# Hybrid decoder layer on one core: rows of chunks 1 to 3 turned by VectorE instead of TensorE, their norm applied at the projections' outputs

## The chip, the cores and the metric

The kernel runs on one core of a Trainium2 chip. The metric is the device time of one execution in microseconds (us), taken as the median of the runs. The core has TensorE for matmuls (PE in the profile; its weight loads stand apart as PEld), VectorE (DVE), ScalarE (ACT), GpSimd (POOL) and SyncE (SP), which here only issues transfers. A transfer is issued by an instruction in the stream of SP, ACT or POOL and is carried out by 16 DMA engines that all of them share. Each engine works through its own instructions in the order in which they were written down.

## The reference

One layer of a decoder, batch 1, 2048 positions, width 1024, all in float32:

```python
h = rms_norm(x, attn_norm_g)                 # over 1024 channels, gain per channel
z = h @ w_in                                 # 1024 -> 2304 columns
q, k, v = z[:512], z[512:640], z[640:768]    # 8 heads of 64, 2 key/value heads
gate_b, gate_c, xc = the last 3 x 512 columns
q, k = rms_norm(q, q_norm_g), rms_norm(k, k_norm_g)
y_attn = sliding-window attention (window 128, one learned sink per head)
y_conv = gate_b * short_conv(gate_c * xc, conv_w)       # causal, 3 taps
x = x + concat(rms_norm(y_attn), rms_norm(y_conv)) @ w_out
x = x + square(relu(rms_norm(x, mlp_norm_g) @ w_up)) @ w_down     # 1024 -> 4096 -> 1024
```

The norm of a row is one number per position, 1/sqrt(mean(x^2) + 1e-6). Called rs below, it may be multiplied into the row ahead of `w_in`, or into the products behind it.

## The kernel before

The positions are cut into four chunks of 512 (`CH`), each of four tiles of 128 positions (`NT`). To keep float32 accuracy every matmul is done as three: each operand is split into a high part (rounded to TensorE's fast float32 format by ScalarE) and a low part (the rest, by VectorE), and `mm3` adds high by high, high by low, low by high (lines 266 to 268).

`mixers(c, ...)` does one chunk of the first half of the layer. Two strands run side by side in it. The one is attention, tile by tile: `scores`, `softmax`, `values`. The other is the generator `besides`, from which `fill(n)` takes n steps between the pieces of attention. Its steps in order: the attention half of the output projection left from the chunk before; two `conv_pair` (matmuls `pc`, `px`, `pb`, with h as the moving operand, so the output has channels on partitions and positions along the row); the convolution half of `out_projection` (`pout<-w_wo,yt`, 96 matmuls), between whose steps `prepare` makes the next chunk's h; then `project_qkv` of the next chunk (`pz`, with h as the stationary operand, so the output has positions on partitions). A planner lays every engine's instructions out in order ahead of time; it goes by the place in the program, shifted by `ahead(i)` by amounts that depend on the chunk, and by when it believes an instruction's inputs to be ready.

h of a chunk lies channels on partitions, in eight blocks k of [128 channels, 512 positions], as a high and a low tile (tags `h0`, `h1`, one buffer each). The next chunk's h can therefore be written only when the last matmul of `conv_pair` (`pb`) has read this chunk's.

For chunk 0 (lines 435 to 540) TensorE turns the raw rows, the gain `g_in` is multiplied in when they are copied out, and rs comes in behind the matmuls: `rs0` as ScalarE's scale where positions lie on partitions, `rs0_row` (VectorE, line 804) where they lie along the row, `rs0_2` (its square) in the norm of the convolution's output.

For chunks 1 to 3 `prepare` (line 363) does four tiles of 128 positions one after the other. `fetch(t)` loads [128, 1024] rows on SP's queue into one of two buffers (line 369), ScalarE squares and sums them (line 275), GpSimd makes rs (lines 190 and 191), and VectorE multiplies by rs and the gain row (line 282). `transposed` (line 288) then lets TensorE turn them in two groups of four 128x128 blocks into the one bank `tr` (line 294), ScalarE copies out the high part (line 298) and VectorE subtracts for the low part (line 299). The rows are already normalized, so `conv_pair` and `project_qkv` copy their products out on ScalarE (lines 802 and 602).

The second half of the layer (products `u` at line 1426 and `d` at line 1533) works on blocks of 512 with seven products in place of eight (Strassen). Its inputs of chunks 2 and 3 are made by `prepare_rest` during the `u` products: `load_turned` loads blocks whose 32x32 squares VectorE's transpose puts in place (`turned`, lines 323 and 324), and the row of rs for them comes by way of DRAM: `rs_out` (line 338) writes it, line 1230 reads it back to all partitions.

Of the kernel before, what the change touches and what calls it, by code (L numbers as in the profile page):

```python
# [70 lines left out]
STEPS = 3  # L71
TS = 32
REST = 7
LATER = 250
# [28 lines left out]
def hymba_layer(  # L103
# [46 lines left out]
    ]  # L150
    rs_dram = [dram.tile([CH], F32, name=f"rs_dram{c}") for c in range(NCHUNK)]
    wds_dram = [[dram.tile([P, 2, BW], F32, name=f"wds{g}_{i}") for i in range(2)] for g in range(NCG // 2)]

    def bank(tag, name):
        return psum.tile([P, 512], F32, tag=tag, name=name, bufs=BANKS[tag])
# [127 lines left out]

    def norm(xt, gb, name):

        scaled(xt, norm_stats(xt, name), gb)

    def transposed(xt, dst, t, name, tag="tr"):

        for kk in range(0, KD, 4):  # L290
            with ahead(9):
                pt = bank(tag, f"pt_{name}_{kk}")
                for j in range(4):
                    nc.tensor.transpose(pt[:, j * P : (j + 1) * P], xt[:, (kk + j) * P : (kk + j + 1) * P], ident)
                p3 = pt.rearrange("p (k t) -> p k t", k=4)
                dh = dst[0][:, kk : kk + 4, t * P : (t + 1) * P]
                dl = dst[1][:, kk : kk + 4, t * P : (t + 1) * P]
                nc.scalar.copy(dh, p3)
                nc.vector.tensor_tensor(dl, p3, dh.bitcast(F32), op=ALU.subtract)
            yield  # L300

    def raised(xt, dst, name, tag="tr"):
# [8 lines left out]

    def load_turned(xb, src, r0, jj):

        for pg in range(4):
            rows = src[r0 : r0 + BW].rearrange("(q i) (k c) -> i k q c", i=TS, k=2)
            c0 = jj * P + pg * TS
            nc.sync.dma_start(
                xb[pg * TS : (pg + 1) * TS].rearrange("p (k q c) -> p k q c", k=2, c=TS), rows[:, :, :, c0 : c0 + TS]
            )

    def turned(xb, k, dst, g, rs_row):

        nc.vector.transpose(dst, xb[:, k * BW : (k + 1) * BW])
        nc.vector.scalar_tensor_tensor(dst, dst, g, rs_row, op0=ALU.mult, op1=ALU.mult)

# [10 lines left out]
    def rs_out(c):  # L336

        nc.gpsimd.dma_start(
            rs_dram[c].rearrange("(t p) -> p t", p=P), rs_x1[:, c * NT : (c + 1) * NT]
        )  # L340
# [21 lines left out]

    def prepare(src, r0, gb, dst, name):

        xs = []

        def fetch(t):
            xt = row("xt", f"xt_{name}_{t}", 2)
            nc.sync.dma_start(xt, src[r0 + t * P : r0 + (t + 1) * P, :])
            with ahead(8):  # L370
                norm(xt, gb, f"{name}_{t}")
                xs.append(xt)

        fetch(0)
        fetch(1)
        yield
        for t in range(NT):
            yield from transposed(xs[t], dst, t, f"{name}_{t}")
            if t + 2 < NT:
                fetch(t + 2)  # L380

# [161 lines left out]
    with tc.tile_pool(name="mix_small", bufs=1) as mix_small, tc.tile_pool(name="mix", bufs=1) as mix:  # L543
# [9 lines left out]
        v_diff = mix.tile([P, KVH * DH], F32, name="v_diff")  # L553
        def project_qkv(c, h, z):

# [37 lines left out]
            for pc, t in ((0, 0), (0, 1), (1, 0), (0, 2), (0, 3), (1, 1), (1, 2), (1, 3)):  # L593
                n = 256 if pc else AW
                ps = bank("mm", f"pz{c}_{pc}_{t}")[:, :n]
                hk = lambda s, k, t=t: h[s][:, k, t * P : (t + 1) * P]
                wk = (lambda s, k: w4[s][:, k, :]) if pc else (lambda s, k: both[k // (KD // 2)][s][:, k % (KD // 2), :])
                for k in range(KD):
                    mm3(ps, lambda s, k=k: hk(s, k), lambda s, k=k: wk(s, k), k == 0, k == KD - 1)
                    if (k % 2 or not pc) and k < KD - 1:  # L600
                        yield
                nc.scalar.copy(z[t][:, pc * AW : pc * AW + n], ps)
                if pc and not t:
                    qk_norm(c * NT, z[0])
                yield
# [171 lines left out]

        def conv_pair(c, h, j, yt, ssc):

# [17 lines left out]
            for i in range(2):  # L797
                ps = bank("mm", f"pc_{nm}_{i}")
                yield from group(hl, ps, i)
                g = pool.tile([P, CHP], F32, tag="s2", name=f"u_{nm}_{i}", bufs=4)  # L800
                if c:
                    nc.scalar.copy(g[:, 2 : CH + 2], ps)
                else:
                    nc.vector.tensor_tensor(g[:, 2 : CH + 2], ps, rs0_row, op=ALU.mult)
                gc.append(g)
                yield
# [132 lines left out]

        def besides(c, before, h, yt, rc, x1, h_next, z_next):  # L940
# [12 lines left out]
            if c + 1 < NCHUNK:  # L953
                h_next += parts(pool, "h", f"h{c + 1}")
                steps = prepare(xf, (c + 1) * CH, g_row[0], h_next, f"a{c + 1}")
            else:
                steps = prepare_mlp(gain_row(mlp_norm_g, "g_mlp"))
            for i, _ in enumerate(steps):
                yield
                for j in range(STEPS):  # L960
                    next(out, None)
                    yield
                    if (i, j) == PC:
# [7 lines left out]
                        with tc.high_priority(offset=SOON):  # L971
                            if c:
                                nc.vector.tensor_copy(ms, pc[:, :NT])
                                rsqrt(rc, ms)
                            else:
                                nc.vector.tensor_tensor(ms, pc[:, :NT], rs0_2, op=ALU.mult)
                                rsqrt(rc, ms)
                                nc.gpsimd.tensor_tensor(rc, rc, rs0, op=ALU.mult)
            yield from out
            if c + 1 < NCHUNK:  # L980
                yield from project_qkv(c + 1, h_next, z_next)
            else:
                begin_mlp()

        def mixers(c, before, h, z):

# [3 lines left out]
            stage[0] = c  # L990
            at, yt, x1, h_next, z_next = [], [], [], [], []
            ra = small.tile([P, NT], F32, tag="ra", name=f"ra{c}", bufs=2)
            rc = small.tile([P, NT], F32, tag="rc", name=f"rc{c}", bufs=2)
            steps = besides(c, before, h, yt, rc, x1, h_next, z_next)
            left = out_projection(c, 0, at, ra, x1)

# [46 lines left out]

            return rest(), h_next, z_next

# [42 lines left out]
        left = iter(())  # L1088
        for c in range(NCHUNK):
            left, h, z = mixers(c, left, h, z)  # L1090
        for _ in left:
# [481 lines left out]
```

## Time and profile before

| | |
|---|---|
| median of 3 runs | 1937.9 us (1937.33 to 1943.99) |
| the profiled execution's own time | 1940.91 us |
| its span, first to last instruction | 1939.2 us |
| granted TensorE clock | 0.997 |
| PE, PEld, DVE, ACT, POOL busy | 99%, 82%, 62%, 43%, 14% of the span |

In the profile, a row of a group gives the line, the engine, the operation, what is written and read, the shape and the count; behind the first bar the busy time and the mean ns of one; behind the second the idle time of that engine right before these instructions and what ended it. Matmuls are pipelined and their ends are modelled, so a PE that is busy 99% still says little: how far apart the starts of its instructions lie says more. Issues of transfers are not counted as busy time. For a transfer, "to landing" is the time from its issue to the signal that it is complete.

### The profile page before, as it was taken

What the parts mean: (1) busy time and instruction counts of PE and PEld (TensorE: products, weight loads), DVE (VectorE), ACT (ScalarE), POOL (GpSimd) and SP (SyncE); (2) the same over time, 40 slices, a digit from 0 to 9 for tenths busy, and PEclk for the clock granted to TensorE, in tenths of its full rate; (3) what the DMA queues carried; (4) which work ended last, traced back from release to release, by engine and by line L of the source; (5) the groups of instructions that cost most, each with busy time, mean ns of one, the idle gap of its engine ahead of it and who ended that gap; (6) DMA issues with size and microseconds to landing.
All of it is one profiled execution on the core that took longest, in us unless ns stands there. A gap on an engine that the chain in (4) does not pass through costs nothing.

```text
span 1939.2 us, 24806 instructions
## 1 busy us (share of the span) xinstructions
PE 1919.0 (99%) x9025; PEld 1597.5 (82%) x9025; DVE 1202.8 (62%) x1872; ACT 837.4 (43%) x1593; POOL 273.5 (14%) x473
## 2 busy tenths in 40 slices
PE   9999999999999999999999999999999999999999
PEld 9888887888888788788877888888888888888887
DVE  4885657447556768888878766666544334448541
ACT  6564444335344436445465555554422332232320
POOL 2122212302221202222200111111000000100000
PEclk9999999999999999999999999999999999999999
DMA  9774854464474788877666544437964446766631
GB/s 334 273 264 140 313 207 174 183 251 152 181 258 159 261 293 259 237 222 245 229 219 202 179 151 148 162 122 293 381 219 142 150 160 233 262 230 215 210 136 54
DMA packets 240634, 412.25 MB, mean 213 GB/s; under 512 B 51704, under 2 KB 147968, under 8 KB 228736
## 3 DMA queue, kind: packets, MB, share of 16 engines
q1 hardware_dynamic: 211824, 335.15, 50.6%
q0 software_dynamic: 15424, 51.40, 7.2%
q10 hardware_dynamic: 13264, 24.13, 3.3%
q8 instruction: 71, 1.16, 0.2%
q14 instruction: 51, 0.42, 0.1%
HBM read 284.78 MB, written 125.83 MB: 212 GB/s over the span
## 4 chain that ended last, share of the span: by engine, by line
PE 85%; issue 5%; DVE 3%; DMA 3%; ACT 2%; POOL 2%; SPq 1%; POOLq 0%; DVEq 0%; ACTq 0%
PE d L1533 31%; PE u L1426 24%; PE pout L266 2%; PE pout L268 2%; PE pout L267 2%; PE pz L266 2%; PE pz L267 2%; PE pz L268 2%; PE pc_c L266 2%; PE px_c L266 2%; PE px_c L268 2%; PE px_c L267 2%; PE pc_c L268 2%; PE pc_c L267 2%; PE psc_b L664 1%
## 5 line engine op out<-in xcount | busy, mean ns | idle before, releaser
L1426 PE MATMUL u<-op_x,wop 128*128 128x512 f32 x2688 | 614.5, 390 | 5.9 <-DVE wop L416 4.4
L1533 PE MATMUL d<-op_w,op_f 128*128 128x512 f32 x2688 | 609.4, 389 | 0.0
L1426 PEld LDWEIGHTS u<-op_x,wop 128*128 128x128 f32 x2688 | 504.7, 188 | 115.2 <-DVE wop L416 7.4
L1533 PEld LDWEIGHTS d<-op_w,op_f 128*128 128x128 f32 x2688 | 504.5, 188 | 104.8
L397 DVE TENSOR_TENSOR op_f<-op_f 128x1024 fp32r<-128x1024 f32 x112 | 136.9, 1225 | 233.8 <-ACT op_f L396 233.3
L396 ACT CAST op_f<-op_f 128x1024 fp32r<-128x1024 f32 x112 | 118.0, 1054 | 349.0 <-DMA op_f<-fop 343.1
L415 ACT CAST wop<-wu 128x512 fp32r<-128x512 f32 x156 | 96.3, 621 | 91.7 <-PE u L1426 88.1
L416 DVE TENSOR_TENSOR wop<-wu,wop 128x512 fp32r<-128x512 f32 x156 | 111.4, 715 | 36.5 <-ACT wop L415 18.8
L1162 POOL DMA_DIRECT2D fop<-s x96 | 52.3, 545 | 440.6 <-DVE s L1165 433.9
L1168 DVE TENSOR_TENSOR u<-u,u 128x512 f32<-128x512 f32 x128 | 87.7, 685 | 20.3 <-PE u L1426 20.3
L397 DVE TENSOR_TENSOR op_w<-raw,op_w 128x1024 fp32r<-128x1024 f32 x56 | 68.4, 1222 | 29.8 <-ACT op_w L396 29.6
L396 ACT CAST op_w<-raw 128x1024 fp32r<-128x1024 f32 x56 | 58.9, 1054 | 48.6 <-PE d L1533 26.6
L1174 ACT ACTIVATE u<-u 128x512 f32<-128x512 f32 x64 | 40.5, 634 | 53.9 <-DVE u L1168 52.0
L681 ACT ACTIVATE sc_b<-sc_b,ngm_b 128x128 f32<-128x128 f32 x128 | 49.8, 394 | 26.5 <-DVE ngm_b L678 26.5
L713 POOL TENSOR_SCALAR_AFFINE_SELECT pp_b<-pp_b 128x512 fp32r<-128x512 f32 x60 | 41.4, 702 | 119.1 <-ACT pp_b L706 64.1
L1375 POOL DMA_DIRECT2D wds<-raw x16 | 8.6, 536 | 332.9 <-DVE raw L1373 332.9
L415 ACT CAST wop<-wu_s 128x512 fp32r<-128x512 f32 x64 | 39.5, 621 | 36.2 <-PE u L1426 28.8
L266 PE MATMUL pout<-w_wo,yt_c 128*128 128x512 f32 x128 | 52.9, 413 | 0.0
L268 PE MATMUL pout<-w_wo,yt_c 128*128 128x512 f32 x128 | 52.4, 409 | 0.0
L267 PE MATMUL pout<-w_wo,yt_c 128*128 128x512 f32 x128 | 51.7, 404 | 0.0
L266 PE MATMUL pout<-w_wo,at_b 128*128 128x512 f32 x128 | 50.2, 394 | 0.2 <-DVE x L891 0.2
L267 PE MATMUL pout<-w_wo,at_b 128*128 128x512 f32 x128 | 50.0, 390 | 0.3 <-DVE w_wo L249 0.3
(255 smaller groups left out, 3126.1 us busy)
## 6 DMA issues: line engine op xcount, KB each, us to landing
op_f<-fop SPq DMA_DIRECT2D x112, 512.0 KB, 4.2
raw<-in_w_down_dram SPq DMA_DIRECT2D x72, 512.0 KB, 4.2
wu<-in_w_up_dram SPq DMA_DIRECT2D x128, 256.0 KB, 3.9
w_wo<-wo SPq DMA_DIRECT2D x24, 1024.0 KB, 6.8
fop<-s POOLq DMA_DIRECT2D x96, 256.0 KB, 2.8
fop<-u ACTq DMA_DIRECT2D x64, 256.0 KB, 2.2
op_x<-xop SPq DMA_DIRECT2D x28, 512.0 KB, 6.6
w_q<-qkv SPq DMA_DIRECT2D x24, 512.0 KB, 6.1
```

Source lines behind the costliest of these rows:

```text
L266: nc.tensor.matmul(ps, st(0), mv(0), start=first, stop=False)
L267: nc.tensor.matmul(ps, st(0), mv(1), start=False, stop=False)
L268: nc.tensor.matmul(ps, st(1), mv(0), start=False, stop=last)
L396: nc.scalar.copy(op[:, 0], raw)
L397: nc.vector.tensor_tensor(op[:, 1], raw, op[:, 0].bitcast(F32), op=ALU.subtract)
L415: splits.append(nc.scalar.copy(hi, blk).ins)
L416: nc.vector.tensor_tensor(lo, blk, hi.bitcast(F32), op=ALU.subtract)
L681: nc.scalar.activation(sc[:, hd, :], sc[:, hd, :], AF.Exp, bias=ngm[:, hd : hd + 1], accum_out=den[:, hd : hd + 1])
L1162: eng.dma_start(fop_dram[tb][ORDER_DOWN.index(i)][n // 2][:, n % 2], b)
L1168: return nc.vector.tensor_tensor(dst, ps, b, op=ALU.add).ins
L1426: nc.tensor.matmul(pt, wops[i][:, a, k, :], xops[tb, p][k // 2][:, b, k % 2, :], start=p not in GOES_ON and k + j == 0, stop=k + j == NB + ...
L1533: nc.tensor.matmul(ps[tb][j], fs[tb][:, a, k, j * P : (j + 1) * P], w[:, b, k, :], start=first and p not in GOES_ON and k + n == 0, stop=l ...
```

## The change

For chunks 1 to 3 the raw rows now go the way of chunk 0, with VectorE in place of TensorE. `load_turned` brings 512 positions by 128 channels in four transfers of 128 KB in pieces of 32 elements; tiles jj = 0 and 1 are issued on SP's queue, 2 and 3 on ScalarE's, once the two `xt` buffers have been read. Per block k, VectorE turns [128, 512] into one half of a new tile `gb`, ScalarE makes the high part times the gain `g_in[k]`, VectorE the low part. rs comes from `stats`, run between the steps of the `conv_pair`s (one step in `STATS` = 9): half rows [128, 512] of the next chunk are loaded on ScalarE's queue into the other half of `gb`, squared and summed in place by ScalarE, and GpSimd makes rs and its square; the square goes to DRAM and comes back as a row to all partitions. `conv_pair` multiplies `pc` by this row on VectorE, for all chunks; `project_qkv` scales by rs on ScalarE; the norm of the convolution's output takes in rs. All rows that go by way of DRAM are now stored partition by partition (`rs_out` too) and read with a step of 4 elements. `norm`, `transposed` and the gain row's load are gone.

```diff
+STATS = 9
-    def transposed(xt, dst, t, name, tag="tr"):
...
-                    nc.tensor.transpose(pt[:, j * P : (j + 1) * P], xt[:, (kk + j) * P : (kk + j + 1) * P], ident)
...
-                nc.scalar.copy(dh, p3)
-                nc.vector.tensor_tensor(dl, p3, dh.bitcast(F32), op=ALU.subtract)
...
-    def load_turned(xb, src, r0, jj):
+    def load_turned(xb, src, r0, jj, eng=None):
...
-            nc.sync.dma_start(
+            (eng or nc.sync).dma_start(
...
         nc.vector.transpose(dst, xb[:, k * BW : (k + 1) * BW])
-        nc.vector.scalar_tensor_tensor(dst, dst, g, rs_row, op0=ALU.mult, op1=ALU.mult)
+        d3, r3 = dst.rearrange("p (t q) -> p t q", t=NT), rs_row.rearrange("p (q t) -> p t q", t=NT)
+        nc.vector.scalar_tensor_tensor(d3, d3, g, r3, op0=ALU.mult, op1=ALU.mult)
...
         nc.gpsimd.dma_start(
-            rs_dram[c].rearrange("(t p) -> p t", p=P), rs_x1[:, c * NT : (c + 1) * NT]
+            rs_dram[c].rearrange("(p t) -> p t", p=P), rs_x1[:, c * NT : (c + 1) * NT]
         )
...
+    def prepare(c, dst, gb):
+        xts = {}
+        def fetch(jj):
+            xts[jj] = row("xt", f"xt_a{c}_{jj}", 2)
+            load_turned(xts[jj], xf, c * CH, jj, nc.scalar if jj > 1 else nc.sync)
         fetch(0)
         fetch(1)
         yield
+        for jj in range(NB):
+            for k in (jj, jj + NB):
+                xt = xts[jj][:, (k // NB) * BW : (k // NB + 1) * BW]
+                with ahead(9):
+                    dh, dl = (d[:, k] for d in dst)
+                    st = gb[:, k // NB]
+                    nc.vector.transpose(st, xt)
+                    nc.scalar.activation(dh, st, AF.Copy, scale=g_in[k])
+                    nc.vector.scalar_tensor_tensor(dl, st, g_in[k], dh.bitcast(F32), op0=ALU.mult, op1=ALU.subtract)
+                yield
+            if jj + 2 < NB:
+                fetch(jj + 2)
+    def stats(c, rs, gb):
+        xr = gb[:, 1]
+        def fetch(t, i):
+            r = c * CH + t * P
+            nc.scalar.dma_start(xr, xf[r : r + P, i * CH : (i + 1) * CH])
+        with tc.issue_after(z_in[-1]) if c == 1 else nullcontext():
+            fetch(0, 0)
+        yield
         for t in range(NT):
...
+            for i in range(2):
+                nc.scalar.activation(xr, xr, AF.Square, scale=D**-0.5, accum_out=ss[:, i : i + 1])
+                if t + i < NT:
+                    fetch(t + i, 1 - i)
+                if i:
+                    nc.gpsimd.tensor_scalar(ss[:, :1], ss[:, :1], EPS, ss[:, 1:], op0=ALU.add, op1=ALU.add)
+                    nc.gpsimd.tensor_tensor(rs[0][:, t : t + 1], ss[:, :1], mhalf[:, :1], op=ALU.pow)
+                yield
+        nc.gpsimd.tensor_tensor(rs[1], rs[0], rs[0], op=ALU.mult)
+        nc.gpsimd.dma_start(rs2_dram[c].rearrange("(p t) -> p t", p=P), rs[1])
...
-                nc.scalar.copy(z[t][:, pc * AW : pc * AW + n], ps)
+                nc.scalar.activation(z[t][:, pc * AW : pc * AW + n], ps, AF.Copy, scale=rs[:, t : t + 1])
...
-                if c:
-                    nc.scalar.copy(g[:, 2 : CH + 2], ps)
-                else:
-                    nc.vector.tensor_tensor(g[:, 2 : CH + 2], ps, rs0_row, op=ALU.mult)
+                t3 = lambda a: a.rearrange("p (t q) -> p t q", t=NT)
+                nc.vector.tensor_tensor(t3(g[:, 2 : CH + 2]), t3(ps), rs2_row, op=ALU.mult)
...
+            gb = pool.tile([P, 2, CH], F32, tag="gb", name=f"gb{c}", bufs=1)
+            rs2_row = rs0_row.rearrange("p (t q) -> p t q", t=NT)
+            if c:
+                nc.sync.dma_start(gb[:, 0], rs2_dram[c].partition_broadcast(P))
+                rs2_row = gb[:, 0].rearrange("p (q t) -> p t q", t=NT)
...
             for j in range(2):
-                yield from conv_pair(c, h, j, yt, ssc)
+                for i, _ in enumerate(conv_pair(c, h, j, yt, ssc, rs2_row)):
+                    if i % STATS == STATS - 1:
+                        next(sums, None)
+                    yield
+            for _ in sums:
+                pass
...
-                            if c:
-                                nc.vector.tensor_copy(ms, pc[:, :NT])
-                                rsqrt(rc, ms)
-                            else:
-                                nc.vector.tensor_tensor(ms, pc[:, :NT], rs0_2, op=ALU.mult)
-                                rsqrt(rc, ms)
-                                nc.gpsimd.tensor_tensor(rc, rc, rs0, op=ALU.mult)
+                            nc.vector.tensor_tensor(ms, pc[:, :NT], rs[1], op=ALU.mult)
+                            rsqrt(rc, ms)
+                            nc.gpsimd.tensor_tensor(rc, rc, rs[0], op=ALU.mult)
...
-        g_row = [gain_row(attn_norm_g, "g_attn")]
```

More of the change, by code (lines that the diff above doesn't have):

```diff
@@ L151, in hymba_layer @@
     rs_dram = [dram.tile([CH], F32, name=f"rs_dram{c}") for c in range(NCHUNK)]
+    rs2_dram = [dram.tile([CH], F32, name=f"rs2_dram{c}") for c in range(NCHUNK)]
     wds_dram = [[dram.tile([P, 2, BW], F32, name=f"wds{g}_{i}") for i in range(2)] for g in range(NCG // 2)]
@@ L776, in attn_rstd, with conv_pair @@
             rsqrt(dst, ms)
-        def conv_pair(c, h, j, yt, ssc):
+        def conv_pair(c, h, j, yt, ssc, rs2_row):
             nm = f"c{c}_{j}"
@@ L1042, in rest @@
                     yield
-            return rest(), h_next, z_next
+            return rest(), h_next, z_next, rs_next
         z = []
```

43 lines of the change are left out of this document (13 added, 30 removed).

## The prediction

> **What bounds the kernel.** I read the page's busy times first, then a table by stretches for the part that the change touches (before about 48 us chunk 0's products start the layer, after 690 us only the second half runs), then who waited for whom on TensorE. A row of the table gives the stretch, its length, and the busy time of each engine in it.
>
> ```profile
> span 1939.2 us, 24806 instructions
> PE 1919.0 (99%) x9025; PEld 1597.5 (82%) x9025; DVE 1202.8 (62%) x1872; ACT 837.4 (43%) x1593; POOL 273.5 (14%) x473
> 48.00:690.00 642.00, 634.93 (x3240) 531.46 (x3239) 417.52 (x835) 295.03 (x794) 134.81 (x226) 1.00 0.60 217
> 123.00:156.00 33.00, 31.95 (x174) 26.62 (x174) 29.89 (x59) 20.66 (x53) 8.01 (x14) 1.00 0.80 275
> 219.00:295.00 76.00, 76.00 (x372) 63.70 (x371) 44.87 (x93) 33.02 (x103) 9.22 (x21) 1.00 0.64 249
> 295.00:329.00 34.00, 32.00 (x170) 26.17 (x169) 25.50 (x53) 17.82 (x50) 9.73 (x15) 1.00 0.47 155
> 466.00:500.00 34.00, 33.04 (x179) 27.17 (x178) 28.75 (x57) 19.08 (x52) 8.87 (x13) 1.00 0.59 202
> ```
>
> TensorE bounds it: in the 642 us of the mixers it is without work for 7. The stretches at 123, 295 and 466 us are those in which the next chunk's h is made; there TensorE is idle for 1 to 2 us, and VectorE is nearly as full as TensorE (29.89 of 33 us at 123, 28.75 of 34 at 466). Between them, as at 219, VectorE has 31 of 76 us to spare. What TensorE waited for, and what the parts that go and come cost:
>
> ```profile
> PE u L1426 <- DVE wop L416: 4.4, 4, 2.9
> PE pt_a L294 <- DVE h_h L299: 1.8, 4, 1.2
> PE po_b L752 <- POOL pp_b L713: 0.3, 1, 0.3
> PE pout L267 <- DVE w_wo L249: 0.3, 1, 0.3
> ```
>
> ```profile
> L294 PE MATMUL pt_a<-ident,xt_a 128*128 128x128 f32 x96 | 14.8, 277 | 4.0 <-DVE h_h L299 1.8 <-DVE ms_b L775 1.2 <-DVE xt_a L282 1.0
> L294 PEld LDWEIGHTS pt_a<-ident,xt_a 128*128 128x128 f32 x96 | 11.2, 140 | 9.0 <-DVE h_h L299 3.7 <-DVE ms_b L775 2.0 <-DVE xt_a L282 1.5
> L282 DVE SCALAR_TENSOR_TENSOR xt_a<-xt_a,rs_a,g_attn 128x1024 f32<-128x1024 f32 x12 | 16.1, 1343 | 5.4 <-POOL rs_a L191 5.4
> L299 DVE TENSOR_TENSOR h_h<-pt_a,h_h 128x512 fp32r<-128x512 f32 x24 | 16.5, 689 | 3.8 <-ACT h_h L298 3.4
> L323 DVE STREAM_TRANSPOSE st_m<-xt_r 128x512 f32<-128x512 f32 x16 | 10.9, 696 | 0.0
> L249 DVE SCALAR_TENSOR_TENSOR w_wo<-raw_wo,g_y,w_wo 128x512 fp32r<-128x512 f32 x16 | 11.6, 745 | 0.0
> L804 DVE TENSOR_TENSOR u_c<-pc_c,rs_row 128x512 f32<-128x512 f32 x4 | 2.8, 688 | 2.2 <-PE pc_c L268 2.2
> L275 ACT ACTIVATE junk_a<-xt_a 128x1024 bf16<-128x1024 f32 x12 | 12.7, 1061 | 6.1 <-DMA xt_a<-in_x_dram 5.4 <-DVE y_c L821 0.4 <-issue 0.2
> L275 ACT ACTIVATION_READ_ACCUMULATOR junk_a<-xt_a 128x1 f32 x12 | 2.3, 190 | 0.0
> L298 ACT CAST h_h<-pt_a 128x512 fp32r<-128x512 f32 x24 | 14.0, 583 | 21.5 <-PE pt_a L294 21.3
> L802 ACT COPY u_c<-pc_c 128x512 f32<-128x512 f32 x12 | 7.1, 589 | 12.6 <-PE pc_c L268 12.4
> L248 ACT ACTIVATE w_wo<-raw_wo,g_y 128x512 fp32r<-128x512 f32 x16 | 10.8, 724 | 0.1
> L766 ACT ACTIVATE o_b<-o_b 128x512 f32<-128x512 f32 x16 | 10.0, 627 | 6.4 <-DVE at_b L765 6.3
> ```
>
> **What TensorE gets back.** The 96 transposes go, in 24 groups of four. What a group takes of TensorE's time is not its 277 ns each, which overlap, but the step between starts:
>
> ```profile
> 123.51 0.39 PE L268 MATMUL pout<-w_wo,yt_c 128*128 128x512 f32 x1
> 123.74 0.60 PE L294 MATMUL pt_a<-ident,xt_a 128*128 128x128 f32 x4
> 124.09 0.48 PE L266 MATMUL pout<-w_wo,yt_c 128*128 128x512 f32 x1
> ```
>
> A matmul of 512 columns holds the place for 0.23 us (123.51 to 123.74), the group of four for 0.35 (to 124.09): 24 x 0.35 = 8.4 us. With them go their waits, 4.0 us on the matmul row; the weight loads waited 9.0, partly beside running matmuls, so 4.0 to 9.0, and I take 4.0. These waits had one cause: a product for the next chunk stood in TensorE's order ahead of ready matmuls and needed a chain over GpSimd, VectorE and the single bank `tr`. In the new order nothing on TensorE touches h before `project_qkv`, so the next thing that can be late is h itself, below.
>
> **The stores by way of DRAM.** One more hole may close. The longest wait in the list above, 2.9 us for `wop`, stands at 776 us, far behind the mixers:
>
> ```profile
> L338 POOL DMA_DIRECT2D rs_dram<-rs_x x2: 851/930/1009, 565.5 to 768.9; - x2
> DMA to landing us min/median/max: 9.0/10.2/11.4
> fop<-s POOLq DMA_DIRECT2D x96, 256.0 KB, 2.8
> 768.91 0.85 POOL L338 DMA_DIRECT2D rs_dram<-rs_x  x1 [0.29 <-POOL rs_x L191]
> 778.19 0.69 DVE L1165 TENSOR_TENSOR s<-f,u 128x512 f32<-128x512 f32 x1 [7.00 <-DMA fop<-s]
> 779.54 0.73 PE L1426 MATMUL u<-op_x,wop 128*128 128x512 f32 x2 [2.93 <-DVE wop L416]
> ```
>
> `rs_out` stores 2 KB as 512 single elements at 768.91 and needs about 10 us to land. The `fop` store issued right behind it, of a kind that lands in 2.8 us, lets VectorE go only at 778.19, 7.0 us late; `wop` stands behind that on VectorE, and TensorE loses 2.93. Stored partition by partition the same row is 128 pieces of 4 elements, a quarter as many. If the delay goes with the pieces, 7.0 becomes 1.8 us, below the 7.0 - 2.9 = 4.1 us that were hidden, and the hole closes: between 0 and 2.9 us won, and I take 2.9, since the only slow store of its kind stands right behind this one. Sum of the gains: 8.4 + 4.0 + 2.9 = 15.3 us.
>
> **What the other engines get.** Per chunk, VectorE loses 4 x 1.343 + 8 x 0.689 = 10.9 us (L282, L299) and gets 8 transposes at 0.696 and 8 low parts at 0.745 (same operation and place as L249), 11.5 us, all in the stretch where h is made, and 4 x 0.688 = 2.8 us in `conv_pair` for what ScalarE copied. The 2.8 lie where 31 of 76 us are free. The +0.6 at 123 us make VectorE's work 29.89 + 0.6 = 30.5 us, while TensorE's, without 8 x 0.35 and the idle 33.00 - 31.95, falls to 33 - 2.8 - 1.0 = 29.2: 1.3 us of that gain cannot be had unless VectorE's work moves out of the stretch. At 295 and 466 us VectorE stays below TensorE (26.1 of 29.2, 29.4 of 30.2). I charge 1.3 us.
>
> The row of rs for chunks 1 to 3 is read with a step of 4 elements, in 12 multiplies and in the 16 of `turned`. No row before shows such a read. Between nothing and a doubling of 0.688 us it is 0 to 28 x 0.69 = 19 us of VectorE, none of it beside a full VectorE; I take 0 for the path. [...]
>
> ScalarE loses, per chunk, 4 x (1.061 + 0.190) + 8 x 0.583 + 4 x 0.589 = 12.0 us. It gets 8 squares of half rows (0.627 as L766, with 0.190 for the sum), 8 high parts with a gain (0.724 as L248), 8 half-row loads and 8 turned loads to issue. For the issues the nearest rows are a plain transfer on ScalarE's queue and the same turned load on SP's; behind each load stands its time to landing, and the last two rows are the plain row loads of `prepare`:
>
> ```profile
> L1162 ACTq DMA_DIRECT2D fop<-u x64: 326/326/393, 752.6 to 1328.3; - x64
> L317 SPq DMA_DIRECT2D xt_r<-x_dram x32: 562/670/3972, 765.2 to 909.1; - x32
> DMA to landing us min/median/max: 2.7/3.6/7.8
> xt_a<-in_x_dram SPq DMA_DIRECT2D x12, 512.0 KB, 5.5
> DMA to landing us min/median/max: 3.2/5.5/12.8
> ```
>
> That is 6.5 + 5.8 + 8 x 0.33 + 8 x 0.67 = 20.3 us, so 8.3 more per chunk, 25 in all, on an engine with 295 of 642 us busy. In the stretches where h is made ScalarE stands at 18 to 21 us of 33 or 34; some 7.2 go (L298 and two squares) and 5.8 + 5.4 come: 22 to 25 of about 30. It fits, but four issues in a row keep ScalarE 2.7 us from attention, whose copies and exponentials stand behind them, and TensorE's order waits for those. This happens at six tiles: between 0 and 6 x 2.7 = 16 us, and I charge 3, near the low end: beside h, the longest waits of TensorE's matmuls in these chunks are the two of 0.3 us in the list above, and the planner has 96 `pout` matmuls and then `pz` to put between. The squares wait for their half rows in ScalarE's order as L275 did for its rows (5.4 us in all, none passed on); they lie in `conv_pair`, where ScalarE is busy 33 of 76 us.
>
> The rest I cost at nothing, each with its cover. SP: 8 turned issues for 4 plain ones and one broadcast, some 4 us per chunk, past the weight loads on its queue; no wait of TensorE in the mixers is on a weight transfer, and if that cover went, each load would be later by at most the eight issues, 5.4 us. DMA engines: the rows are read twice, half of them in pieces of 128 bytes; their share is 0.60 over the mixers. GpSimd: as many small operations as before and one store per chunk, on a queue with no other store there until chunk 3. The read-back of the row waits for that store, but has until the first `pc` group ends, 24 matmuls or 5.5 us after `conv_pair` begins, and two more banks. `project_qkv` copies with a scale in place of a plain copy.
>
> **Sum.** 15.3 - 1.3 - 3 = 11.0 us. Against the profiled execution's own 1940.9 us (its span and 1.7 us around it) that gives 1929.9; its time lies 3.0 above the median of the runs, so the median of the changed kernel should be 1937.9 - 11.0 = 1926.9 us, 0.57% less. Half a percent, 9.7 us, is about what a measurement of this kernel can tell from no change: faster means under 1928.2, slower over 1947.6.
>
> **Rivals.** First, ScalarE's issues are passed on in full: 15.3 - 1.3 - 16 = -2.0, 1939.9 us, no change. For it speaks the 3.97 us that one such issue once took on SP; against it, the 10 us or more that ScalarE has free in these stretches. The same verdict, with 1926.9 + 2.9 = 1929.8, comes if only the hole at 776 us stays, that is if the slow store has another cause.
>
> Second, and on the other side: the late tiles hold up VectorE. Tiles 2 and 3 of a chunk are loaded only when their buffers have been read, while `pout` runs. If one lands later than the planner believed, the transpose at the head of VectorE's order stands, and behind it the additions that free `pout`'s banks. Three banks of 12 matmuls give 2 x 12 x 0.23 = 5.5 us of cover; every microsecond over that is lost, six times. At the typical landing of 3.6 us nothing is lost. At the worst of the rows above, 12.8, a tile would be 12.8 - 3.6 = 9.2 us late and cost 3.7: 6 x 3.7 = 22 us, 1949 us. It decides from (11.0 + 9.7) / 6 = 3.5 us each, a landing of 12.6 us. For it: the DMA share of 0.80 at 123 us. Against it: none of the 16 transposes L323 shows an idle VectorE before it. [...]
>
> Third, h comes too late as a whole. Before, `project_qkv` began while the last tiles were still being turned:
>
> ```profile
> 328.53 0.40 PE L266 MATMUL pz<-w_q,h_h 128*128 128x512 f32 x1
> 330.39 0.60 PE L294 MATMUL pt_a<-ident,xt_a 128*128 128x128 f32 x4
> ```
>
> Now its first group reads all eight blocks k, so h must be whole. After the last `pb`, two blocks (2.9 us of VectorE), four issues (2.7), a landing (3.6 to 7.8) and two more blocks with a high part (3.6) make 13 to 17 us of the 29 that TensorE has other work for. Only with a landing near 20 us does it cost; then each microsecond costs three.
>
> **How the numbers follow.** The forecast 0.50, ScalarE or the hole 0.24, late tiles 0.21, late h 0.05. Half of the last stays within half a percent. So faster 0.50, within 0.5% 0.26, slower 0.24. The time is the forecast's, 1926.9. Its own range is 1919 (the waits at 9.0, no charge for ScalarE) to 1930 (hole stays). For 8 in 10 the range takes in the first rival and the late tiles up to their price: 1918 to 1949 us.
>
> **What would show it.** Right: no `pt_a` at all in the mixers; TensorE's idle time over them down by some 4 us and the mixers shorter by 10 to 12; `rs_dram` landing well under 9 us and no 2.9 us hole behind it. Wrong: waits of DVE on `xt_a` transfers, ScalarE busy with issues above 0.7 us each ahead of `sc`, `pp` or `qt`, or TensorE waiting for `h_h` at the first `pz`.

## The result, and the profile after

The changed kernel takes 1999.4 us, the median of four runs; four runs of the kernel before beside it have a median of 1939.5. The ratio is 1.030, with a 95% interval of 1.029 to 1.032: 3% slower, where 0.57% less was forecast and 1949 us was the upper end of the range. The profiled execution took 1995.4 us, 1993.7 of it span.

First, the page's busy times after:

```profile
span 1993.7 us, 24735 instructions
PE 1940.2 (97%) x8929; PEld 1597.8 (80%) x8929; DVE 1220.5 (61%) x1896; ACT 837.2 (42%) x1605; POOL 272.0 (14%) x482
```

And rows of the table by stretches (length, then busy time of PE, PEld, DVE, ACT and POOL, granted clock, DMA share, GB/s), two of them before, then after:

```profile
48.00:123.00 75.00, 75.00 (x367) 62.69 (x366) 63.09 (x130) 42.66 (x118) 10.15 (x18) 1.00 0.70 259
156.00:219.00 63.00, 62.73 (x334) 53.38 (x334) 34.64 (x67) 28.16 (x65) 21.21 (x32) 1.00 0.56 173
```

```profile
48.00:123.00 75.00, 60.62 (x291) 50.26 (x290) 45.70 (x95) 33.32 (x98) 15.43 (x23) 0.89 0.64 208
156.00:219.00 63.00, 54.73 (x278) 45.70 (x277) 36.39 (x76) 29.39 (x74) 15.54 (x24) 0.96 0.69 188
400.00:466.00 66.00, 61.88 (x286) 51.04 (x285) 39.55 (x83) 25.48 (x79) 15.02 (x27) 0.96 0.63 223
48.00:690.00 642.00, 604.36 (x2965) 503.41 (x2964) 395.64 (x811) 278.83 (x777) 127.97 (x225) 0.97 0.63 212
```

TensorE has 96 matmuls fewer and is busy 21 us longer. Over the 642 us from 48 to 690, which were the mixers before, it lacks work for 38 us, where it lacked 7, and its clock is 0.97 of full speed there, where it was 1.00. Most of the loss isn't where h is made. It is in the stretch from 48 us, when chunk 0's `conv_pair` runs and chunk 1's statistics beside it, and again at the statistics of chunks 2 and 3.

Second, who waited for whom: TensorE's longest waits after, and ScalarE's for the half rows (us in total, times, longest).

```profile
PE ptq_b L651 <- ACT sc_b L686: 14.4, 1, 14.4
PE pout L268 <- DVE x L903: 6.3, 6, 2.7
PE po_b L766 <- POOL pp_b L727: 6.2, 2, 5.7
PE u L1446 <- ACT wop L429: 3.9, 2, 3.1
PE pz L268 <- ACT z L616: 2.0, 1, 2.0
ACT gb L386 <- DMA gb<-in_x_dram: 59.1, 18, 9.3
```

The first row is the hole of 14.4 us. The timeline around it (start, length, and in brackets the idle time before it and what ended it) shows what ScalarE was doing:

```profile
65.24 0.34 ACTq L378 DMA_DIRECT2D gb<-in_x_dram  x1
...
74.94 0.63 ACT L386 ACTIVATE gb<-gb 128x512 f32<-128x512 f32 x1 [7.07 <-DMA gb<-in_x_dram]
75.70 0.34 ACTq L378 DMA_DIRECT2D gb<-in_x_dram  x1
...
84.94 0.63 ACT L386 ACTIVATE gb<-gb 128x512 f32<-128x512 f32 x1 [9.27 <-DMA gb<-in_x_dram]
85.69 0.37 ACT L686 COPY sc_b<-psc_b 128x256 f32<-128x256 f32 x1
86.12 0.47 PE L651 MATMUL ptq_b<-ident,z 128*128 128x128 f32 x1 [14.38 <-ACT sc_b L686]
```

A half row is asked for at 65.24 and its square starts at 74.94. Only then is the buffer free to ask for the next, at 75.70, and its square starts at 84.94. Attention's copy of the scores, L686, stands behind both in ScalarE's order. It runs at 85.69, and TensorE, which needs the bank that it empties, goes on at 86.12.

The next largest holes are the same wait, seen through other engines. At 212.88 us another square starts, 6.98 us late:

```profile
212.88 0.63 ACT L386 ACTIVATE gb<-gb 128x512 f32<-128x512 f32 x1 [6.98 <-DMA gb<-in_x_dram]
213.72 0.30 POOL L390 TENSOR_SCALAR ss_a<-ss_a 128x1 f32<-128x1 f32 x1 [8.00 <-ACT gb L386]
214.63 1.23 POOL L727 TENSOR_SCALAR_AFFINE_SELECT pp_b<-pp_b 128x512 fp32r<-128x512 f32 x2
215.32 1.38 PE L766 MATMUL po_b<-pp_b,vd 128*128 128x512 f32 x2 [5.69 <-POOL pp_b L727]
...
399.26 0.63 ACT L386 ACTIVATE gb<-gb 128x512 f32<-128x512 f32 x1 [1.69 <-DMA gb<-in_x_dram]
400.02 0.71 DVE L365 STREAM_TRANSPOSE gb<-xt_a 128x512 f32<-128x512 f32 x1 [11.57 <-ACT gb L386]
```

GpSimd had the sum of that square (L390) ahead of attention's mask (L727) in its order, stood 8.00 us for it, and TensorE lost 5.69. In chunk 2 VectorE stood 11.57 us: its first transpose for h writes into `gb`, the tile that the statistics were still using. TensorE's holes of 1.6 and 2.7 us at 405 and 412 us, waiting for VectorE, come right behind that.

These holes cost twice, because the granted clock drops to half behind them. Five stretches of the table after, each beginning in or right behind a hole:

```profile
74.40:91.30 16.90, 5.18 (x15) 3.97 (x16) 5.20 (x15) 4.30 (x15) 1.06 (x3) 0.50 0.68 191
214.40:221.00 6.60, 5.68 (x24) 5.29 (x25) 6.07 (x11) 6.04 (x14) 3.72 (x5) 0.50 0.13 41
340.60:347.40 6.80, 6.38 (x24) 5.35 (x24) 5.10 (x16) 0.84 (x5) 1.49 (x3) 0.50 0.24 37
415.80:419.10 3.30, 3.30 (x9) 2.59 (x8) 2.41 (x6) 0.00 (x0) 0.96 (x1) 0.50 0.00 0
524.90:528.30 3.40, 3.19 (x8) 2.52 (x9) 2.81 (x7) 1.30 (x7) 0.41 (x2) 0.50 0.02 5
```

From 86.1 to 91.4 TensorE works at half speed, a loss of 2.7 us, then 2.9 from 215.3 to 221.1, and 1.7 each at 399 and 416. The stretches at 340.6 and 524.9, some 5 us lost, are not behind half rows: they stand where h is made, behind holes of 0.9 to 1.3 us, and come back under "h not ahead".

Where the 54.5 us of span went follows from the first matmul of the second half, at 695.0 us before and 736.9 after. The mixers lost 41.9 us and the second half, which the change hardly touches, the remaining 12.6. This is what its matmuls show, before and then after:

```profile
L1426 PE MATMUL u<-op_x,wop 128*128 128x512 f32 x2688 | 614.5, 390 | 5.9 <-DVE wop L416 4.4 <-ACT wop L415 1.0 <-ACT u L1181 0.4
L1533 PE MATMUL d<-op_w,op_f 128*128 128x512 f32 x2688 | 609.4, 389 | 0.0
```

```profile
L1446 PE MATMUL u<-op_x,wop 128*128 128x512 f32 x2688 | 624.9, 394 | 4.7 <-ACT wop L429 3.9 <-DVE wop L430 0.8
L1553 PE MATMUL d<-op_w,op_f 128*128 128x512 f32 x2688 | 613.7, 391 | 0.0
```

The same 2688 + 2688 matmuls, at a clock of 1.00, are busy 10.4 and 4.3 us longer without waiting more. From start to start a u matmul takes 227 ns before; after, most take some 233.

### The profile page after: what moved, and what is told of

Its sections match the earlier page's. It is cut to its first block, busy times and chain, and to the rows that moved or that the text cites. A ratio compares the mean times of both kernels' runs of the same rounds, so it can differ in the third digit from the quotient of the medians.

```text
span 1993.7 us, 24735 instructions
## 1 busy us (share of the span) xinstructions
PE 1940.2 (97%) x8929; PEld 1597.8 (80%) x8929; DVE 1220.5 (61%) x1896; ACT 837.2 (42%) x1605; POOL 272.0 (14%) x482
## 4 chain that ended last, share of the span: by engine, by line
PE 78%; DMA 6%; DVE 5%; issue 5%; ACT 3%; POOL 2%; SPq 1%; ACTq 0%; POOLq 0%; DVEq 0%
PE d L1553 31%; PE u L1446 25%; DMA gb<-in_x_dram 4%; PE pout L268 2%; PE pout L269 2%; PE pout L270 2%; PE pb_c L270 1%; PE pc_c L268 1%; PE pc_c L270 1%; PE pc_c L269 1%; PE pb_c L269 1%; PE pb_c L268 1%; PE px_c L270 1%; PE pz L268 1%; PE px_c L268 1%
## 5 line engine op out<-in xcount | busy, mean ns | idle before, releaser
L1446 PE MATMUL u<-op_x,wop 128*128 128x512 f32 x2688 | 624.9, 394 | 4.7 <-ACT wop L429 3.9
L429 ACT CAST wop<-wu 128x512 fp32r<-128x512 f32 x156 | 96.2, 620 | 101.5 <-PE u L1446 97.8
L727 POOL TENSOR_SCALAR_AFFINE_SELECT pp_b<-pp_b 128x512 fp32r<-128x512 f32 x60 | 39.8, 676 | 119.9 <-ACT pp_b L720 60.0
L429 ACT CAST wop<-wu_s 128x512 fp32r<-128x512 f32 x64 | 39.5, 620 | 38.7 <-PE u L1446 35.1
```

Source lines behind the costliest of these rows:

```text
L429: splits.append(nc.scalar.copy(hi, blk).ins)
L1446: nc.tensor.matmul(pt, wops[i][:, a, k, :], xops[tb, p][k // 2][:, b, k % 2, :], start=p not in GOES_ON and k + j == 0, stop=k + j == NB + ...
```

## The experiments

Two things had to be explained: the mixers, and matmuls that got slower though nothing about them was changed. For the second there was one suspect. The change replaces some tiles in the pool `small`, and everything allocated behind that pool (weights, `wop`, four of the operand tiles of the second half) moves by 128 bytes per partition, while tiles allocated from the other end stay. All kernels below that differ only in such a shift have every engine's order of the kernel that they start from.

**Placement.** The kernel before, with 128 bytes of padding, as the change has it:

```diff
-    both_pool = ctx.enter_context(tc.tile_pool(name="both", bufs=1, reuse_waits="tile"))
+    small.tile([P, 32], F32, name="pad"); both_pool = ctx.enter_context(tc.tile_pool(name="both", bufs=1, reuse_waits="tile"))
```

> The kernel before with 128 bytes more per partition in its pool of small tiles, so that every tile behind it stands where the changed kernel has it (18944 becomes 19072, the first weight tile); nothing else differs, the order of all engines is the same. Theory 'place' (the matmuls of the second half take 231 instead of 226 ns because their operands no longer begin on a multiple of 256 bytes): the step of the u matmuls goes from 226 to 231 or 232 ns, the second half gets 12 us longer (u) and 4 (d), the mixers some 5, in all 1955 to 1962. Theory 'transfers' (the longer steps come from other traffic in the changed kernel): 1937 to 1943, step 226.

Measured: 1956.1 us against 1940.0, ratio 1.0084 (1.0065 to 1.0103). The page's rows for the two kinds of matmul:

```profile
L1426 PE MATMUL u<-op_x,wop 128*128 128x512 f32 x2688 | 625.6, 394 | 5.4 <-DVE wop L416 3.4 <-ACT wop L415 2.1
L1533 PE MATMUL d<-op_w,op_f 128*128 128x512 f32 x2688 | 613.6, 390 | 0.0
```

These are the changed kernel's numbers, so 16 us of its loss are an address. The mixers hardly felt it (first u matmul at 695.9 us): there, by the kernel's pools, both operands of a matmul moved together. The trace holds no addresses, but the kernel says which matmul has an operand in a tile that moved. Sorted by that, the starts in this trace show the same thing: u matmuls whose two operands have the same remainder by 256 bytes take 228 ns from start to start, those with a difference of 128 bytes 233; d matmuls 227 and 232.5, whichever of the two operands is the moved one. A shift of 128 bytes that both share costs 1 ns at most.

The reverse, the changed kernel with 384 bytes more, so that all remainders are those of the kernel before:

```diff
-    both_pool = ctx.enter_context(tc.tile_pool(name="both", bufs=1, reuse_waits="tile"))
+    small.tile([P, 96], F32, name="pad"); both_pool = ctx.enter_context(tc.tile_pool(name="both", bufs=1, reuse_waits="tile"))
```

> The changed kernel with 384 bytes more in the pool of small tiles, so that the tiles behind it stand 512 bytes further than in the kernel before (19456 for 18944) and the remainders are the same. Theory 'place': the u and d matmuls are back at 226 ns, 16 us in the second half and some 5 in the mixers come back, 1999 becomes 1976 to 1984; the stall at 71 us and the clock behind it stay. Theory 'transfers': 1995 to 2000, step 232.

Measured: 1977.9 us, ratio to before 1.0194 (1.0173 to 1.0215). By the profiled executions 16.7 us came back (a span of 1977.0 for 1993.7); the u matmuls are busy 613.1 us, the d matmuls 609.4. The hole is still there, 14.2 us long. Two more shifts of the kernel before, one execution each:

> The kernel before with 256 bytes more in the pool of small tiles; the order of all engines is that of the kernel before. The weights wop and four of the moving operands are then 256 bytes off the others' remainder by 512. Theory 'remainder by 256 counts': u matmuls at 226.. 227 ns, 1937 to 1944. Theory 'remainder by 512 counts': some 232 ns where the two operands differ, as with 128 bytes, 1952 to 1960.

> As the one before with 64 bytes. Theory 'any difference of the remainders counts': 1952 to 1960, at least 5 ns more per u matmul whose operands differ. Theory 'only 128 counts': 1937 to 1944.

```profile
L1426 PE MATMUL u<-op_x,wop 128*128 128x512 f32 x2688 | 613.2, 390 | 6.3 <-DVE wop L416 5.4 <-ACT wop L415 0.6 <-ACT u L1181 0.2
```

```profile
L1426 PE MATMUL u<-op_x,wop 128*128 128x512 f32 x2688 | 627.7, 394 | 5.8 <-DVE wop L416 3.9 <-ACT wop L415 1.9
```

With 256 bytes nothing is lost (the first row, 1942.4 us); with 64 it is as much as with 128 (the second, 1959.4 us). So far as these shifts show, what counts is whether the addresses of the two operands have the same remainder by 256 bytes. Why pairs with different remainders take longer, no run shows.

**Half rows.** From here on all kernels made from the changed one have the 384 bytes. The statistics read whole rows, two ahead, into the two tiles `xt` that stand free until the turned tiles need them:

```diff
-        xr = gb[:, 1]
...
-            nc.scalar.dma_start(xr, xf[r : r + P, i * CH : (i + 1) * CH])
...
+            xr[t] = row("xt", f"xr_a{c}_{t}", 2)
+            nc.sync.dma_start(xr[t], xf[c * CH + t * P : c * CH + (t + 1) * P, :])
...
-                nc.scalar.activation(xr, xr, AF.Square, scale=D**-0.5, accum_out=ss[:, i : i + 1])
...
+            nc.scalar.activation(xr[t], xr[t], AF.Square, scale=D**-0.5, accum_out=ss)
+            if t + 2 < NT:
+                fetch(t + 2)
```

> As the one before (512 bytes further), and the statistics read whole rows into the two tiles of 1024 columns that stand free until the turned tiles come, two rows ahead, issued by SP; ScalarE makes 4 squares of 1024 columns a chunk in place of 8 of 512, each of which waited for a load that could only begin behind the square before it. Theory 'half rows' (ScalarE's order stands at a square whose half row was only just asked for, and attention's copies stand behind it): ScalarE's waits for these loads fall from 59 us to under 15, the hole of 14 us at 71 us goes, and the mixers get 25 to 40 us shorter: 1938 to 1955. Theory 'turned tiles' (the turned loads that ScalarE issues are what delays it): no more than 5 us gained, 1973 to 1982.

Measured: 1943.4 us, ratio to before 1.0020 (1.0010 to 1.0031), so 34.5 us less than with half rows. ScalarE's row for the squares:

```profile
L386 ACT ACTIVATE xr_a<-xr_a 128x1024 f32<-128x1024 f32 x12 | 12.7, 1056 | 2.7 <-DMA xr_a<-in_x_dram 2.5
```

ScalarE's wait falls from 60.8 to 2.5 us, and the hole at 71 us is gone. The sum is near the reading of the trace: holes of 14.4, 5.7, 2.0, 1.6 and 2.7 us with half clock of 2.7, 2.9, 1.7 and 1.7 behind them make 35.4. That it is so near is partly luck. Some 5 us of smaller holes (at 153 to 163 and at 243 us) went too, and rows ahead has a new hole of 2.5 us at 112 us with 6.8 us of half clock behind it, some 6 us; the two about cancel. This run changes three things at once, though: the depth, the size and the place of the loads, and the planner laid out the order of all engines anew, as it did for the next kernel. In its timeline chunk 1's squares run at 40 to 55 us, before the weight loads that the half rows met at 65 to 85. So one more kernel kept half rows, issued by ScalarE, and only gave them two tiles in turn:

```diff
-        xr = gb[:, 1]
...
+            xr[n] = row("xt", f"xr_a{c}_{n}", 2)[:, :CH]
...
+                if n + 2 < 2 * NT:
+                    fetch(n + 2)
```

> The changed kernel, 512 bytes further, with the half rows still half rows and still issued by ScalarE, but in two tiles in turn (those of the turned tiles), each asked for two squares ahead. Theory 'one buffer' (each load could only start when the square before it had run, so that the whole time to landing, 3 to 10 us, stood in ScalarE's order): ScalarE's waits for half rows fall from 60 us to under 20, 1977 becomes 1940 to 1952. Theory 'eight loads and their place' (whole rows or SP's queue made the difference): ScalarE still waits over 40 us, 1965 to 1980.

```profile
ACT xr_a L389 <- DMA xr_a<-in_x_dram: 26.9, 11, 7.2
PE ptk_b L656 <- ACT sc_b L689: 5.4, 1, 5.4
PE ptq_b L654 <- ACT sc_b L689: 4.4, 1, 4.4
```

Measured: 1966.0 us, ratio 1.0126 (1.0111 to 1.0141): the time at the lower end of the second expectation, the wait between the two. The wait is less than half, 26.9 us, and 12 us are won. But these loads still need up to 10.9 us to land; those of chunk 1 are asked for up to 74 us, among weight loads that SP issues from 59 to 72 us, and two buffers don't cover that. By these two runs the single buffer is a third of the loss; the rest goes with size, queue and place together, and these were not taken apart.

**Who issues the turned tiles.** All of them from SP instead of half from ScalarE, once in the changed kernel and once with rows ahead:

```diff
-            load_turned(xts[jj], xf, c * CH, jj, nc.scalar if jj > 1 else nc.sync)
+            load_turned(xts[jj], xf, c * CH, jj, nc.sync)
```

> The changed kernel, 512 bytes further, with all turned tiles issued by SP and none by ScalarE; half rows as in the change. Theory 'half rows': within 8 us of the second run of this group, 1970 to 1990, and ScalarE still waits some 50 us for half rows. Theory 'turned tiles': 24 issues of 0.59 us and what stands behind them leave ScalarE, and the mixers get 20 us or more shorter, under 1960.

> The kernel with rows ahead, and all turned tiles issued by SP. Theory 'the issues on ScalarE cost little once the half rows are gone' (the prediction charged 3 us): 1940 to 1946. Theory 'they still cost 2.7 us at each of six tiles': 1930 to 1936.

Measured: 1991.8 us (1.0268, 1.0249 to 1.0288) and 1974.7 us (1.0169, 1.0142 to 1.0195), 14 and 31 us slower than the kernels that they start from. In the first ScalarE still waits 66.9 us for half rows, so its issues of turned tiles aren't what delays those. (Whether the turned loads themselves, whoever issues them, slow the half rows was not tested. The half row asked for at 65.24 in the changed kernel was late before the first of them was issued, at 74.98.) Neither expectation foresaw a loss of this size. In both runs the planner has laid out the order of all engines anew. In the first run three of the new holes stand behind half rows again, of 6.7, 10.1 and 6.7 us; one of them, with the square that was late and the TensorE operation behind it:

```profile
192.65 0.63 ACT L386 ACTIVATE gb<-gb 128x512 f32<-128x512 f32 x1 [6.31 <-DMA gb<-in_x_dram]
194.83 1.69 PE L766 MATMUL po_b<-pp_b,vz 128*128 128x512 f32 x2 [6.70 <-ACT pp_b L720]
```

In the second, TensorE's new holes are mostly waits for VectorE (`ssc`, `z`, `pp_b`), and not for a transfer. The runs therefore don't price the issues; they show that issuing from ScalarE is no worse here than the planner's answer to taking them away. Why the second run's order is so much worse stays open.

**The step in the row of rs squared.** With rows ahead, and the row stored as 512 single elements, the multiplies of `conv_pair` read it without a step; the order of all engines is the same:

```diff
-        nc.gpsimd.dma_start(rs2_dram[c].rearrange("(p t) -> p t", p=P), rs[1])
+        nc.gpsimd.dma_start(rs2_dram[c].rearrange("(t p) -> p t", p=P), rs[1])
...
-                rs2_row = gb[:, 0].rearrange("p (q t) -> p t q", t=NT)
+                rs2_row = gb[:, 0].rearrange("p (t q) -> p t q", t=NT)
```

> The kernel with rows ahead, and rs squared of chunks 1 to 3 stored as 512 single elements, so that the 12 multiplies of conv_pair read their row without a step; the order of all engines is that of the kernel with rows ahead. These multiplies go from 1062 to some 690 ns. Theory 'strided reads cost the path' : at least 2 us of the mixers come back, 1939 to 1942. Theory 'VectorE has room there': no difference, 1942 to 1945, or up to 3 us slower if the store of single elements lands too late for the first multiply of a chunk.

The row with the step of 4 (rows ahead), and without it (this run):

```profile
L814 DVE TENSOR_TENSOR u_c<-pc_c,gb 128x512 f32<-128x512 f32 x12 | 12.7, 1062 | 9.9 <-PE pc_c L270 9.8
```

```profile
L814 DVE TENSOR_TENSOR u_c<-pc_c,gb 128x512 f32<-128x512 f32 x12 | 8.3, 688 | 10.2 <-PE pc_c L270 10.1
```

Measured: 1943.4 us, ratio to before 1.0014 (1.0002 to 1.0027), the same as with the step (1.0020). A strided multiply costs 374 ns more, 4.4 us in all, and none of it can be told in the time.

**The store alone.** The kernel before with `rs_out` stored partition by partition and the strided read in `turned` that goes with it, nothing else, in the same order:

```diff
-            rs_dram[c].rearrange("(t p) -> p t", p=P), rs_x1[:, c * NT : (c + 1) * NT]
+            rs_dram[c].rearrange("(p t) -> p t", p=P), rs_x1[:, c * NT : (c + 1) * NT]
```

> The kernel before with one part of the change alone: the row of rs for the second half is stored partition by partition (128 pieces of 4 elements for 512 single ones) and so read with a step of 4 by the 16 multiplies of the turned tiles. The order of all engines is that of the kernel before. Theory 'pieces' (the prediction's): the store lands in under 5 us for 9.0, the fop store behind it no longer holds VectorE, the hole of 2.9 us at 776 us closes, 1.5 to 4 us won, and the 16 multiplies (1187 ns for 798 in the changed kernel) lose nothing: 1935 to 1939. Theory 'another cause': the hole stays within 1 us, 1938 to 1944.

```profile
770.14 0.64 POOL L339 DMA_DIRECT2D rs_dram<-rs_x  x1 [0.29 <-POOL rs_x L191]
770.78 1.07 POOL L1163 DMA_DIRECT2D fop<-s  x2
773.13 0.69 DVE L1166 TENSOR_TENSOR s<-f,u 128x512 f32<-128x512 f32 x1 [0.70 <-DMA fop<-s]
```

Measured: 1937.6 us against 1941.4, ratio 0.9978 (0.9965 to 0.9991). VectorE waits 0.70 us where it waited 7.00, and TensorE has no hole over 1.2 us after 10 us. The 3.7 us are more than the hole of 2.9, which in the kernel before had half clock right behind it:

```profile
780.60:784.00 3.40, 3.40 (x10) 2.62 (x9) 3.35 (x6) 0.21 (x1) 1.08 (x2) 0.50 0.71 184
```

The 16 multiplies take 1188 for 798 ns; no loss from them can be seen.

**h not ahead.** What is left with rows ahead are holes of 2.5, 1.3 and 0.8 us at 112, 314 and 484 us, each followed by 6.8 us at half clock. One of them in the timeline, and the stretch behind it:

```profile
314.92 1.05 PE L989 MATMUL pc<-mean,ssc 128*128 128x1 f32 x8 [1.30 <-DVE ssc L852]
```

```profile
316.00:322.60 6.60, 6.21 (x19) 5.07 (x20) 5.11 (x16) 1.95 (x11) 2.28 (x5) 0.50 0.12 18
```

Here the last addition to `ssc` stands on VectorE behind two operations for the next h (L367), which the planner puts ahead. The changed kernel has the same at 339 us, with the half clock at 340.6. The kernel without that, and one without it in chunks 1 and 2 only:

```diff
-    (40, 0, 160, -10, 10, 0, 80, 10, -20, 30, 0, 300),
-    (220, 0, -60, -50, 40, 0, 270, -20, 50, 280, 0, 0),
-    (200, 0, 10, -50, 40, 0, 260, -20, 70, 280, 0, 10),
+    (40, 0, 160, -10, 10, 0, 80, 10, -20, 0, 0, 300),
+    (220, 0, -60, -50, 40, 0, 270, -20, 50, 0, 0, 0),
+    (200, 0, 10, -50, 40, 0, 260, -20, 70, 0, 0, 10),
```

> The kernel with rows ahead, and the planner no longer puts the turning of tiles for h (3 operations a block) ahead of chunk c's own work (30, 280, 280 become 0). Theory 'VectorE's load where h is made' (the holes of 1.3 us at 313 and 1 us at 483, where ssc and kw stand behind three operations of h, and the 6.8 us of half clock after each): the holes and the half clock at 316 and 487 go, 4 to 9 us won, 1935 to 1940. Theory 'h then comes too late': TensorE waits for h_h at the first pz of a chunk, 1945 to 1965.

> The kernel with rows ahead; the tiles for h are not put ahead in chunks 1 and 2 (280 becomes 0) and stay so in chunk 0 (30). Theory: the holes of 1.0 and 1.7 us that the run without any of them has at 48 and 51 us are not there, the rest stays as in that run: 1927 to 1931. If those holes have another cause: 1931 to 1934.

The same three stretches with rows ahead, and then without h ahead:

```profile
123.00:156.00 33.00, 31.67 (x154) 25.59 (x153) 29.86 (x56) 20.25 (x53) 4.36 (x7) 1.00 0.87 290
295.00:329.00 34.00, 31.66 (x143) 25.72 (x142) 26.25 (x54) 17.97 (x50) 6.57 (x10) 0.90 0.45 128
466.00:500.00 34.00, 32.44 (x147) 26.52 (x147) 26.72 (x56) 17.82 (x48) 6.65 (x11) 0.90 0.47 134
```

```profile
123.00:156.00 33.00, 33.00 (x163) 27.00 (x162) 29.43 (x54) 20.34 (x53) 4.65 (x7) 1.00 0.93 307
295.00:329.00 34.00, 33.10 (x166) 27.83 (x165) 25.93 (x56) 15.32 (x44) 8.95 (x13) 1.00 0.55 158
466.00:500.00 34.00, 34.00 (x170) 28.44 (x169) 27.86 (x59) 17.65 (x50) 8.38 (x14) 1.00 0.67 218
```

Measured: 1932.1 us, ratio 0.9952 (0.9937 to 0.9967), and 1934.0, ratio 0.9957 (0.9940 to 0.9973). The first is the fastest of all: the change with its placement, its statistics and its priorities mended beats the kernel before by half a percent. 11.2 us, more than the 4 to 9 expected, came from three numbers in a table and the order that the planner made of them, by way of waits of about a microsecond and the clock behind them: of the three stretches at half clock in the mixers the two at 316 and 487 us are gone (a clock of 1.00 where it was 0.90, in the rows above). The holes at 48 and 51 us, which the second kernel was to remove, did go, but others of about 1 us came at 119 and 148: the same within what can be told.

## Why the prediction was wrong

**Transposes, 8.4 us: right.** There is no `pt_a` of chunks 1 to 3 in the trace. From start to start these 96 instructions took 9.1 us of TensorE in the trace before.

**Waits before L294, 4.0 us: gone as said, but not kept.** The prediction said that what can be late next is h itself. What was late were the statistics.

**The hole at 776 us, 2.9 us: right.** Alone it gives 3.7 us. The changed kernel has a hole of 3.1 us nearby, but with another cause: ScalarE starts the split of an `op_x` block 3.49 us late because its load had not landed, and L429 stands behind it.

**VectorE, charge 1.3 us: too low, though its mechanism was named.** Where h is made VectorE is nearly as full as TensorE; with rows ahead, no longer putting h in front of VectorE's other work gave 11 us, since the holes of about 1 us that this left had half clock behind them. The strided reads at 0 for the path: right.

**ScalarE, charge 3 us, 0 to 16: here the prediction failed**, in the sentence "The squares wait for their half rows in ScalarE's order as L275 did for its rows (5.4 us in all, none passed on)". They waited 59.1 us, and some 35 us were passed on. L275's rows were loaded two tiles ahead by SP; a half row can be asked for only when the square before it has left the single buffer, so its landing, 2.8 us in the median and up to 9.7, stands in ScalarE's order. The prediction had the row that showed such landings (up to 12.8 us for the row loads) and used it only for the turned tiles. That ScalarE was busy 33 of 76 us was no cover: attention's copies stand in the same order, and while ScalarE waited for a half row they waited too.

**SBUF placement, 16 us: missing from the prediction**, which has no term for where the tiles lie. It also had none for the clock behind a hole, though the trace before has 3.4 us of half clock twice, at 671 us and, as shown above, at 780.

**The rivals.** The first looked at ScalarE's order and the second at a load that holds an engine in its order; the loss was both, but with the half rows as the load. What ScalarE's issues cost stays open. No DVE wait on an `xt_a` transfer and no late `h_h` at `pz` appears. From the measured 1999.4 the kernels lead back, each compared with the one ahead of it: 21.5 us for placement, 34.5 for the half rows, 11.2 for h, which leaves 1932.1, 5 us above the forecast of 1926.9. Of the 21.5, only 16 are explained: that is what the shift alone costs the kernel before, and 16.7 is the difference of the profiled executions. And the kernel before took 1941.4 us beside the last kernel, so that it wins 9.2 us of the 11.0 forecast. The store alone wins 3.7 of these, which leaves 5.5 us for everything else, forecast at 8.1.

## What to carry to other kernels

When a change puts a load in front of an operation on an engine that runs in order, ask first how many of these loads can be under way at once, and take the worst landing in the trace, not the typical one; here, with one buffer and landings of up to 9.7 us, ScalarE stood still for 59.1 us, and so did what stood behind it in its order. When tiles are added to a pool or taken from it, look at the addresses of everything behind it: here 384 bytes of padding, which made the shift 512 bytes, brought back 16.7 us. And an order that a planner lays out anew with each edit is part of the edit: change one thing in a way that keeps the order, or compare the orders before explaining the time.

## What the runs showed of the hardware

Matmuls of 128 x 512 in float32 took 231 to 234 ns from start to start instead of 227 when one operand had been moved by 128 bytes and the other not, and 227 or 228 when neither or both had (the kernel before with 128 bytes, and the changed kernel's trace in groups of 12 matmuls); at full clock, in the `u` and `d` matmuls of the second half. In the kernel before, the 2688 `u` and 2688 `d` matmuls were busy 614.5 and 609.4 us; with a shift of 64 bytes it was 627.7 and 612.6, with 128 it was 625.6 and 613.6, with 256 it was 613.2 and 609.4.

With rows ahead, a hole of 1.3 us on TensorE at 314 us, with 0.4 us shortly ahead of it, was followed by 6.8 us at half clock, and so was one of 0.8 at 484 us with 0.3 behind it; in both places `pc` matmuls of a single column run next to the hole. Half clock came in stretches of 3.4 or 6.8 us, and of 17.1 us in the changed kernel from within the hole of 14.4 us on. Other holes of over 1 us (before, 1.05 us long at 145 us and 1.22 at 309 us) had a clock of 1.00 behind them, so the length of one hole alone does not decide. What does, no run shows.
